# A transformer trunk on one core: layer 1's seven-product blocks put in written order, raw weights asked for earlier, and the fourth token sum moved among the first block

## The chip, the cores and the metric

The kernel runs on one core of a Trainium2 chip. The engines of the core are PE (matrix products, with its weight loads as PEld), DVE (vector), ACT (scalar and activations), POOL (a second vector engine that cannot read the product banks) and SP, which here only issues transfers. They run side by side, each through its own row of instructions, and wait for one another by semaphores. The metric is the device time of one execution in microseconds (us); lower is better. A run is stated as the median of several executions.

## The reference, cut to what matters

The model has two layers over 1024 latent tokens of width 1024. Each layer ends with a feed-forward part:

```python
def _mlp(h, w1, w2):
    return jnp.square(jax.nn.relu(h @ w1)) @ w2
...
x = x + gx2 * _mlp(_modulate(_rms(x, norm_mlp_g[i]), sx2, cx2), mlp_w1[i], mlp_w2[i])
```

`w1` is 1024 x 4096 and `w2` 4096 x 1024, all in float32. What changes lies wholly in layer 1's `_mlp`, the last part of the program.

## The kernel before

Every float32 operand of a product is held as two parts, a high part and the rest (names that end in `h` and `l`; the weights' two parts lie side by side in one tile `wsp` of 128x1024). A product of two operands is three matmuls: high by high, high by low, low by high.

Layer 1's feed-forward part has 32 feature tiles of 128. The first four go the plain way (`mlp`, whose last rows are issued by `first_done`). The other 28 go in 14 blocks, `units` 2 to 15, of two feature tiles each. A block computes its `h @ w1` as a 2x2 by 2x2 product of quarters (two feature tiles by two halves of the inner dimension, times two halves of the inner dimension by two halves of the tokens, `H0` and `H1`) with seven quarter products in place of eight. For that the tokens' quarters are combined beforehand into sums (`token_sums`: tiles t1, t2 in the buffers `oh`, `ol`, and one quarter of `mh`, `ml` overwritten; `token_sum_4`: tiles `t4`), and the weights' quarters are combined in every block (`make_s2`, four DVE operations). A quarter product (`product`) is 12 matmuls of 128x512. Below they are called P0 (`unit_head`) and P1 to P6 (`unit_tail`, in the order written); they go into three banks a, b and c. Banks are read between the products: `s1` is a copy of bank a after P0, `u2` and `u3` are bank b plus `s1`, and `added` makes the quarters c22, c21 and c12. Each of the four result quarters then goes through `squared`: a ReLU and a square on ACT (`uh`), a square on POOL, a difference on DVE (`ul`). `unit_down` multiplies the block's 256 features by `w2`: 16 banks of six matmuls, each added to the stream by one DVE operation (`residual`, L311). A block is thus 84 + 96 = 180 matmuls of 128x512.

Weights come in as raw float32 tiles of 128x1024 (`raw`, three buffers; two per block from `w1`, L1413, two from `w2`, L1435) and are cut into eleven pieces per block by `fresh`: a cast on ACT (L247), then a subtraction on POOL (L248). `makers` lists the pieces in the order of their use, `make(4)` keeps four of them made, and the tiles have four buffers: a new piece can be cast only when the piece four places before it has been used up by PE.

What sets the order: the program is written as one sequence, and a scheduler then places each engine's instructions by its own estimate of times. Only what stands in `with in_order()` keeps the written sequence, engine by engine. Before the change the blocks do not stand in it, so the scheduler interleaves products of neighbouring stages. Where a raw tile is asked for is also part of the sequence: `make_a11`, `make_s2` and `make_down` ask for it just ahead of its use. The four `token_sum_4` are written between `unit_head` of the first block and the first `unit_tail`.

## Time and profile before

| | us |
|---|---|
| median of 3 runs | 2735.89 (2733.7 to 2740.11) |
| the profiled execution: its time | 2737.96 |
| its span, by the profile | 2736.1 |
| PE busy / PEld busy | 2638.0 / 2186.3 |
| DVE / ACT / POOL busy | 1665.2 / 913.9 / 1017.1 |

Times in the rows count from the start of the span. A busy time says how long an engine had something in work, not whether it was waited for; matmuls overlap, so a single one is shown as 0.39 us long though one starts every 0.23 us. The blocks run from 2133 us to the end.

### The profile page before, as it was taken

How to read it: one execution, taken by the hardware profiler on the slowest of the kernel's cores; microseconds unless marked ns; L12 is line 12 of the kernel's file. 1: busy time of each engine (PE TensorE's matmuls, PEld its weight loads, DVE VectorE, ACT ScalarE, POOL GpSimd, SP SyncE). 2: the span in 40 equal slices, each digit the busy share in tenths (PEclk: the TensorE clock that was granted, in tenths of full speed). 3: DMA queues.
4: the chain of work that ended last, by engine and by line, in shares of the span. 5: the costliest groups of instructions: out<-in, count | busy, mean ns of one | idle time of the engine just before them, and what ended most of it. 6: DMA issues, size and time to landing. Idle time of an engine off the chain costs nothing.

```text
span 2736.1 us, 37282 instructions
## 1 busy us (share of the span) xinstructions
PE 2638.0 (96%) x13787; PEld 2186.3 (80%) x13787; DVE 1665.2 (61%) x3623; ACT 913.9 (33%) x1988; POOL 1017.1 (37%) x838
## 2 busy tenths in 40 slices
PE   7989799999999999999899999999989899999999
PEld 5878687888888888888688887788868778788787
DVE  5778779455464554624962535888877645545545
ACT  4211246121221211213532225766744232232322
POOL 3323256332332322323411002544466454454543
PEclk9999899999999999999999999999999999999999
DMA  7233420222222222311333334534221111111112
GB/s 251 72 115 124 132 82 16 63 92 81 81 96 73 85 84 78 97 43 46 97 119 116 122 118 138 166 101 136 92 66 39 39 60 48 47 55 39 62 46 85
DMA packets 148937, 239.44 MB, mean 88 GB/s; under 512 B 10460, under 2 KB 91644, under 8 KB 148756
## 3 DMA queue, kind: packets, MB, share of 16 engines
q1 hardware_dynamic: 147316, 234.45, 26.8%
q8 instruction: 108, 1.77, 0.3%
q10 hardware_dynamic: 1440, 2.62, 0.2%
q14 instruction: 73, 0.60, 0.1%
HBM read 208.71 MB, written 28.32 MB: 87 GB/s over the span
## 4 chain that ended last, share of the span: by engine, by line
PE 72%; DVE 9%; issue 3%; DMA 2%; POOL 2%; ACT 1%; DVEq 0%; POOLq 0%; SPq 0%; ACTq 0%
PE ps L295 16%; PE ps L294 16%; PE ps L296 16%; PE ps L1464 5%; PE ps L1152 3%; PE ps L1154 3%; PE ps L1153 3%; PE ps L102 3%; PE ps L1288 3%; DMA raw<-in_mlp_w_dram 2%; PE ps L1105 2%; DVE junk L218 1%; POOL wsp L248 1%; PE ps L1107 1%; DVE ny L373 1%
## 5 line engine op out<-in xcount | busy, mean ns | idle before, releaser
L248 POOL TENSOR_TENSOR wsp<-raw,wsp 128x512 fp32r<-128x512 f32 x355 | 500.0, 1413 | 938.0 <-ACT wsp L247 904.4
L311 DVE SCALAR_TENSOR_TENSOR xT<-ps,mods,xT 128x512 f32<-128x512 f32 x528 | 367.0, 711 | 308.8 <-PE ps L296 308.3
L247 ACT CAST wsp<-raw 128x512 fp32r<-128x512 f32 x368 | 224.5, 619 | 758.6 <-PE ps L296 538.7
L295 PE MATMUL ps<-ul,wsp 128*128 128x512 f32 (+1 forms) x1280 | 473.5, 370 | 1.7 <-DVE ul L1470 0.8
L218 DVE CUSTOM_DVE_ANT_0 junk<-raw,cond_b 128x256 bf16<-128x256 f32 x640 | 354.8, 554 | 192.6 <-DMA raw<-in_ada_t_dram 92.7
L296 PE MATMUL ps<-uh,wsp 128*128 128x512 f32 (+1 forms) x1280 | 468.4, 368 | 0.0
L294 PE MATMUL ps<-uh,wsp 128*128 128x512 f32 (+1 forms) x1280 | 458.9, 369 | 0.5 <-ACT wsp L247 0.5
L295 PE MATMUL ps<-ml,wsp 128*128 128x512 f32 (+1 forms) x792 | 285.5, 361 | 11.1 <-DVE ml L408 7.5
L294 PE MATMUL ps<-mh,wsp 128*128 128x512 f32 (+1 forms) x792 | 284.6, 361 | 1.2 <-ACT mh L401 1.2
L296 PE MATMUL ps<-mh,wsp 128*128 128x512 f32 (+1 forms) x792 | 283.7, 359 | 0.0
L295 PEld LDWEIGHTS ps<-ul,wsp 128*128 128x128 f32 x1280 | 241.4, 189 | 47.0 <-DVE ul L1470 7.2
L294 PEld LDWEIGHTS ps<-uh,wsp 128*128 128x128 f32 x1280 | 241.4, 189 | 41.9 <-ACT wsp L247 0.9
L296 PEld LDWEIGHTS ps<-uh,wsp 128*128 128x128 f32 x1280 | 241.2, 188 | 40.0
L966 POOL TENSOR_TENSOR tmp<-tmp 128x512 f32<-128x512 f32 (+1 forms) x104 | 103.8, 999 | 217.8 <-ACT tmp L963 189.6
L295 PEld LDWEIGHTS ps<-ml,wsp 128*128 128x128 f32 x792 | 151.1, 191 | 37.4 <-DVE ml L408 10.8
L294 PEld LDWEIGHTS ps<-mh,wsp 128*128 128x128 f32 x792 | 151.0, 191 | 24.6 <-ACT mh L401 1.4
L296 PEld LDWEIGHTS ps<-mh,wsp 128*128 128x128 f32 x792 | 151.2, 191 | 21.4
L1464 PE MATMUL ps<-mh,wsp 128*128 128x512 f32 x448 | 148.1, 397 | 14.0 <-ACT ny L1481 7.2
L963 ACT ACTIVATE tmp<-ps 128x512 f32<-128x512 f32 (+1 forms) x104 | 55.3, 532 | 257.7 <-PE ps L296 257.2
L967 DVE TENSOR_TENSOR ul<-tmp,uh 128x512 fp32r<-128x512 f32 (+1 forms) x104 | 90.5, 875 | 80.8 <-POOL tmp L966 80.8
L294 PE MATMUL ps<-hh,wsp 128*128 128x512 f32 (+1 forms) x360 | 130.0, 361 | 1.9 <-ACT wsp L247 1.6
L295 PE MATMUL ps<-hl,wsp 128*128 128x512 f32 (+1 forms) x360 | 129.5, 360 | 2.0 <-DVE hl L408 1.3
(335 smaller groups left out, 5079.0 us busy)
## 6 DMA issues: line engine op xcount, KB each, us to landing
raw<-in_mlp_w_dram SPq DMA_DIRECT2D x92, 512.0 KB, 3.5
raw<-in_ada_t_dram SPq DMA_DIRECT2D x80, 512.0 KB, 3.5
raw<-in_mlp_w_dram SPq DMA_DIRECT2D x80, 256.0 KB, 2.7
raw<-in_w_qkv_dram SPq DMA_DIRECT2D x24, 512.0 KB, 4.0
k_d<-tmp SPq DMA_DIRECT2D x40, 256.0 KB, 2.4
kh<-k_d SPq DMA_DIRECT2D x15, 640.0 KB, 5.0
kl<-k_d SPq DMA_DIRECT2D x15, 640.0 KB, 6.9
araw<-in_ada_dram SPq DMA_DIRECT2D x16, 512.0 KB, 9.6
```

Source lines behind the costliest of these rows:

```text
L102: PE.transpose(dst, src, ident[:rows, :rows])
L218: DVE.tensor_tensor_reduce(out=junk, in0=raw[:, d * 256:d * 256 + 256], in1=cond_b[:, s, :], op0=ALU.mult, op1=ALU.add, scale=1.0, scalar= ...
L247: ACT.copy(dst_hi, src)
L248: lo_eng.tensor_tensor(out=dst_lo, in0=src, in1=dst_hi.bitcast(F32), op=ALU.subtract)
L294: PE.matmul(ps, lhsT=whi, rhs=ahi, start=first, stop=False)
L295: PE.matmul(ps, lhsT=whi, rhs=alo, start=False, stop=False)
L296: PE.matmul(ps, lhsT=wlo, rhs=ahi, start=False, stop=last)
L311: DVE.scalar_tensor_tensor(out=xT[dt][ci], in0=ps, scalar=mods[l][:, 24 * k + 16 + dt, s:s + 1], in1=xT[dt][ci], op0=ALU.mult, op1=ALU.add)
L966: POOL.tensor_tensor(out=q[:, :w], in0=r[:, :w], in1=r[:, :w], op=ALU.mult)
L967: DVE.tensor_tensor(out=ul[:, off:off + w], in0=q[:, :w], in1=hs.bitcast(F32), op=ALU.subtract)
L1152: PE.matmul(ps, lhsT=ah, rhs=wh, start=(kt == 0), stop=False)
L1464: PE.matmul(ps, lhsT=a, rhs=b, start=(first and kt == 0 and n == 0), stop=(kt == 3 and n == 2), skip_group_check=True)
```

## The change

Four things are done, all in layer 1's feed-forward part.

1. All blocks stand in `with in_order()`: each engine takes their instructions as written.
2. Raw tiles are asked for earlier: `make_s1`, `make_a22`, `make_s4` and `make_down(i, 1)` issue the transfers of `up_raw(i + 1, 0)`, `down_raw(i, 0)`, `down_raw(i, 1)` and `up_raw(i + 1, 1)`; the first block's two are asked for inside `first_done`.
3. The four `token_sum_4` are written among the first `unit_tail`, one `step()` after each of u2, the first `squared`, u3 and c22.
4. One subtraction of `token_sum_4` goes from DVE to POOL, and in the first block P6 (`p3`, which needs no t4) is written ahead of P5 (`p4`), with the two weight pieces swapped to match.

```diff
@@ token_sum_4
-        DVE.tensor_tensor(out=f21, in0=f21, in1=f2, op=ALU.subtract)
+        POOL.tensor_tensor(out=f21, in0=f21, in1=f2, op=ALU.subtract)
@@ raw tiles
     def up_raw(i, j):
-        raws[i, j] = raw_w()
-        SP.dma_start(raws[i, j], mlp_w1[1][2 * i + j])
-
-    def make_a11(i):
-        up_raw(i, 0)
-        return fresh(raws[i, 0][:, H0])
+        if i in units:
+            raws[i, j] = raw_w()
+            SP.dma_start(raws[i, j], mlp_w1[1][2 * i + j])
+
+    def down_raw(i, j):
+        raws["d", i, j] = raw_w()
...
     def make_s2(i):
-        up_raw(i, 1)
...
     def make_down(i, j):
-        if j % 2 == 0:
-            raws["d", i] = raw_w()
...
+        w = fresh(raws["d", i, j // 2][:, 512 * (j % 2):512 * (j % 2) + 512])
+        if j == 1:
+            up_raw(i + 1, 1)
+        return w
+
+    def make_s1(i):
+        up_raw(i + 1, 0)
+        return fresh(sums_.pop(i))
+
+    def make_a22(i):
+        w = fresh(raws.pop((i, 1))[:, H1])
+        down_raw(i, 0)
+        return w
+
+    def make_s4(i):
+        w = fresh(raws.pop((i, 0))[:, H0])
+        down_raw(i, 1)
+        return w
@@ unit_tail
+        late = [lambda kt=kt: token_sum_4(kt) for kt in range(4)] if opens else []
+        step = lambda: late.pop(0)() if late else None
         product(b, pair_of(tsum["t2"]), True)
         DVE.tensor_tensor(out=u2, in0=b, in1=s1, op=ALU.add)
+        step()
+        us = [(big("uh"), big("ul")) for _ in range(2)]
         product(a, quarter(upper, H0), False)
         squared(tmp(), *us[0], H0, a)
+        step()
         product(b, quarter(lower, H1), False)
         DVE.tensor_tensor(out=u3, in0=b, in1=s1, op=ALU.add)
+        step()
         product(c, pair_of(tsum["t1"]), True)
         c22 = added(c, u3)
+        step()
         squared(c22, *us[1], H1, c22)
...
+        for p in (p3, p4) if opens else (p4, p3):
+            p()
@@ the end of the program
-    head = unit_head(units[0])
-    for kt in range(4):
-        token_sum_4(kt)
-    for i in units:
-        us = unit_tail(head)
-        if i + 1 in units:
-            head = unit_head(i + 1)
-        unit_down(us, store if i + 1 not in units else None)
+    with in_order():
+        head = unit_head(units[0])
+        for i in units:
+            us = unit_tail(head, i == units[0])
+            if i + 1 in units:
+                head = unit_head(i + 1)
+            unit_down(us, store if i + 1 not in units else None)
```

How this moves the instructions shows at three places. First PE inside an ordinary block, before the change. `oh` is t1 (P4), `t` is t4 (P5); the first `mh`, `ml` here are the last rows of P3, and the two after `oh` are the first rows of the next block's P0; `uh`, `ul` belong to `unit_down`.

```order
L1464 MATMUL ps<-mh_17799,wsp 128x512
L1464 MATMUL ps<-oh,wsp 128x512
L1464 MATMUL ps<-mh_17796,wsp 128x512
L1464 MATMUL ps<-ml_17804,wsp 128x512
L1464 MATMUL ps<-t_18828,wsp 128x512 x3
L1464 MATMUL ps<-t_18836,wsp 128x512 x3
L1464 MATMUL ps<-t_18844,wsp 128x512 x3
L1464 MATMUL ps<-t_18852,wsp 128x512 x3
L294 MATMUL ps<-uh,wsp 128x512
L295 MATMUL ps<-ul,wsp 128x512
```

The same place after it:

```order
L1482 MATMUL ps<-mh_17799,wsp 128x512
L1482 MATMUL ps<-oh,wsp 128x512 x12
L1482 MATMUL ps<-t_18850,wsp 128x512 x3
L1482 MATMUL ps<-t_18884,wsp 128x512 x3
L1482 MATMUL ps<-t_18910,wsp 128x512 x3
L1482 MATMUL ps<-t_18935,wsp 128x512 x3
L1482 MATMUL ps<-mh_17800,wsp 128x512
L1482 MATMUL ps<-ml_17808,wsp 128x512
```

P4 now stands in one piece, P5 follows it, and neither the next P0 nor `unit_down` reaches in between.

Second, ACT at the start of the first block, before the change (`wsp_18808` and `wsp_18811` are weight pieces of P2 and P3, `ny_18826` is s1):

```order
L247 CAST wsp_18808<-raw_18791 128x512
L247 CAST t4_18828<-tmp_18829 128x512
L247 CAST t4_18836<-tmp_18837 128x512
L247 CAST t4_18844<-tmp_18845 128x512
L247 CAST wsp_18811<-raw_18796 128x512
L247 CAST t4_18852<-tmp_18853 128x512
L1481 COPY ny_18826<-ps_18807 128x512
```

And after it (`wsp_18834`, `wsp_18862`, `wsp_18892` are the pieces s1, s4 and a22):

```order
L247 CAST wsp_18808<-raw_18721 128x512
L247 CAST wsp_18811<-raw_18723 128x512
L1499 COPY ny_18826<-ps_18807 128x512
L247 CAST wsp_18834<-tmp_18798 128x512
L247 CAST t4_18850<-tmp_18851 128x512
L247 CAST wsp_18862<-raw_18721 128x512
L1485 ACTIVATE tmp_18879<-ps_18807 128x512
L1486 ACTIVATE uh_18858<-tmp_18879 128x512
L247 CAST t4_18884<-tmp_18885 128x512
L247 CAST wsp_18892<-raw_18723 128x512
L247 CAST t4_18910<-tmp_18911 128x512
```

The copy of bank a no longer stands behind the casts of t4; those now stand between the casts of the block's own pieces.

Third, DVE in the first block. Before the change the sums of t4 stand ahead of the block, which then reads:

```order
L248 TENSOR_TENSOR t4_18852<-tmp_18853,t4_18852 128x512
L1489 TENSOR_TENSOR ny_18866<-ps_18864,ny_18826 128x512
L1470 TENSOR_TENSOR ul_18861<-tmp_18899,uh_18860 128x512
L1493 TENSOR_TENSOR ny_18867<-ps_18864,ny_18826 128x512
L1474 TENSOR_TENSOR tmp_18937<-ps_18865,ny_18867 128x512
```

After it (L1509 is u2, L1516 u3, L1492 c22; L1372 adds the two parts of a t2 tile, L248 makes the low part of a t4 tile):

```order
L1509 TENSOR_TENSOR ny_18830<-ps_18828,ny_18826 128x512
L1372 TENSOR_TENSOR tmp_18853<-ol_18494 128x512
L248 TENSOR_TENSOR t4_18850<-tmp_18851,t4_18850 128x512
L1488 TENSOR_TENSOR ul_18859<-tmp_18879,uh_18858 128x512
L1372 TENSOR_TENSOR tmp_18887<-ol_18544 128x512
L248 TENSOR_TENSOR t4_18884<-tmp_18885,t4_18884 128x512
L1516 TENSOR_TENSOR ny_18831<-ps_18828,ny_18826 128x512
L1372 TENSOR_TENSOR tmp_18913<-ol_18594 128x512
L248 TENSOR_TENSOR t4_18910<-tmp_18911,t4_18910 128x512
L1492 TENSOR_TENSOR tmp_18933<-ps_18829,ny_18831 128x512
```

Three of the four token sums now stand on DVE between u2 and c22.

## Rows read from the trace of the kernel before

**Rows 1.** PE in time: start, length, line, operation, count; rows around P0 and P1.

```profile
2119.72 0.39 PE L294 MATMUL ps<-uh,wsp 128*128 128x512 f32 x1
...
2133.09 0.39 PE L296 MATMUL ps<-uh,wsp 128*128 128x512 f32 x1
2133.32 0.39 PE L1464 MATMUL ps<-mh,wsp 128*128 128x512 f32 x1
...
2136.04 0.61 PE L1464 MATMUL ps<-ol,wsp 128*128 128x512 f32 x2
2137.02 2.58 PE L1464 MATMUL ps<-ol,wsp 128*128 128x512 f32 x10 [0.36 <-POOL wsp L248]
2146.79 0.79 PE L1464 MATMUL ps<-mh,wsp 128*128 128x512 f32 x1 [7.19 <-ACT ny L1481]
...
2151.64 0.40 PE L1464 MATMUL ps<-mh,wsp 128*128 128x512 f32 x1
...
2731.95 0.39 PE L296 MATMUL ps<-uh,wsp 128*128 128x512 f32 x1
```

**Rows 2.** Busy time by stretch: PE, PEld, DVE, ACT, POOL; granted clock, DMA, GB/s.

```profile
2147.00:2149.00 2.00, 2.00 (x5) 1.61 (x6) 0.57 (x1) 0.77 (x2) 1.67 (x2) 0.50 0.00 0
2153.00:2155.00 2.00, 2.00 (x10) 1.64 (x10) 0.00 (x0) 0.78 (x2) 1.67 (x2) 1.00 0.00 1
```

**Rows 3.** The chain of waits: start, length, what; the same cast in the first and the last block.

```profile
2157.37 0.63 ACT wsp L247
...
2704.17 0.63 ACT wsp L247
```

**Rows 4.** PE in time, in the second of the 14 blocks.

```profile
2199.29 0.39 PE L1464 MATMUL ps<-oh,wsp 128*128 128x512 f32 x1
2200.21 0.50 PE L1464 MATMUL ps<-mh,wsp 128*128 128x512 f32 x1 [0.53 <-ACT wsp L247]
...
2214.87 0.50 PE L295 MATMUL ps<-ul,wsp 128*128 128x512 f32 x1
```

**Rows 5.** DVE in time, the same block.

```profile
2209.59 0.75 DVE L1423 TENSOR_TENSOR tmp<-raw 128x512 f32<-128x512 f32 x1 [0.95 <-DMA raw<-in_mlp_w_dram]
...
2214.13 0.69 DVE L1470 TENSOR_TENSOR ul<-tmp,uh 128x512 fp32r<-128x512 f32 x1
2214.73 4.70 DVE L311 SCALAR_TENSOR_TENSOR xT<-ps,mods,xT 128x512 f32<-128x512 f32 x7
```

**Rows 6.** ACT in time: first block's start, then the second block's casts and activations.

```profile
2145.63 0.62 ACT L247 CAST t<-tmp 128x512 fp32r<-128x512 f32 x1 [5.99 <-DVE tmp L1396]
2146.16 0.58 ACT L1481 COPY ny<-ps 128x512 f32<-128x512 f32 x1
...
2204.44 0.63 ACT L1467 ACTIVATE tmp<-tmp 128x512 f32<-128x512 f32 x1
```

**Rows 7.** DVE in time while the token sums run.

```profile
2132.88 0.68 DVE L1372 TENSOR_TENSOR tmp<-ol 128x512 f32<-128x512 f32 x1
...
2141.99 1.75 DVE L1372 TENSOR_TENSOR tmp<-ol 128x512 f32<-128x512 f32 x1
```

**Rows 8.** POOL in time, the same stretch and on.

```profile
2134.43 1.30 POOL L1372 TENSOR_TENSOR tmp<-mh,ml 128x512 f32<-128x512 f32 x1 [3.29 <-DVE tmp L1396]
...
2139.80 3.38 POOL L248 TENSOR_TENSOR wsp<-raw,wsp 128x512 fp32r<-128x512 f32 x2
...
2154.58 1.04 POOL L1469 TENSOR_TENSOR tmp<-tmp 128x512 f32<-128x512 f32 x1
```

**Rows 9.** PE in time after another long idle stretch, in layer 0.

```profile
185.86 0.79 PE L294 MATMUL ps<-yh,wsp 128*128 128x512 f32 x1 [7.85 <-ACT wsp L247]
...
188.58 0.59 PE L295 MATMUL ps<-yl,wsp 128*128 128x512 f32 x1
189.01 0.40 PE L294 MATMUL ps<-yh,wsp 128*128 128x512 f32 x1
```

**Rows 10.** Line L1413, the 28 raw tiles of w1: us from issue to landing.

```profile
DMA to landing us min/median/max: 3.3/3.5/4.2
```

More of the change, by code (lines that the diff above doesn't have):

```diff
@@ L1411, in up_raw @@
     def up_raw(i, j):
-        raws[i, j] = raw_w()
-        SP.dma_start(raws[i, j], mlp_w1[1][2 * i + j])
-    def make_a11(i):
-        up_raw(i, 0)
-        return fresh(raws[i, 0][:, H0])
+        if i in units:
[3 more added lines that the diff above has]
+        raws["d", i, j] = raw_w()
+        src = mlp_w2[1, i // 2, 4 * j:4 * j + 4, :, 256 * (i % 2):256 * (i % 2) + 256]
+        SP.dma_start(raws["d", i, j].rearrange("p (m c) -> p m c", m=4), src.rearrange("m p c -> p m c"))
     def make_s2(i):
-        up_raw(i, 1)
         r1, r2 = raws[i, 0], raws[i, 1]
@@ L1431, in make_down @@
     def make_down(i, j):
-        if j % 2 == 0:
-            raws["d", i] = raw_w()
-            src = mlp_w2[1, i // 2, 2 * j:2 * j + 4, :, 256 * (i % 2):256 * (i % 2) + 256]
-            SP.dma_start(raws["d", i].rearrange("p (m c) -> p m c", m=4), src.rearrange("m p c -> p m c"))
-        return fresh(raws["d", i][:, 512 * (j % 2):512 * (j % 2) + 512])
+        w = fresh(raws["d", i, j // 2][:, 512 * (j % 2):512 * (j % 2) + 512])
[13 more added lines that the diff above has]
+        return w
     units = range(2, 16)
     for i in units:
-        makers.append(lambda i=i: make_a11(i))
+        makers.append(lambda i=i: fresh(raws[i, 0][:, H0]))
         if i > units[0]:
@@ L1445, in trunk @@
         makers.append(lambda i=i: fresh(raws[i, 1][:, H0]))
-        makers.append(lambda i=i: fresh(sums_.pop(i)))
-        makers.append(lambda i=i: fresh(raws.pop((i, 1))[:, H1]))
-        makers.append(lambda i=i: fresh(raws.pop((i, 0))[:, H0]))
+        makers.append(lambda i=i: make_s1(i))
+        if i == units[0]:
+            makers.append(lambda i=i: make_s4(i))
+            makers.append(lambda i=i: make_a22(i))
+        else:
+            makers.append(lambda i=i: make_a22(i))
+            makers.append(lambda i=i: make_s4(i))
     makers.extend(lambda j=j: make_down(units[-1], j) for j in range(4))
@@ L1482, in unit_head, with unit_tail, p4, p3 @@
         return a, s1
-    def unit_tail(head):
+    def unit_tail(head, opens):
         a, s1 = head
-        us = [(big("uh"), big("ul")) for _ in range(2)]
         b, c, u2, u3 = bank(), bank(), keep(), keep()
+        late = [lambda kt=kt: token_sum_4(kt) for kt in range(4)] if opens else []
+        step = lambda: late.pop(0)() if late else None
         product(b, pair_of(tsum["t2"]), True)
         DVE.tensor_tensor(out=u2, in0=b, in1=s1, op=ALU.add)
+        step()
+        us = [(big("uh"), big("ul")) for _ in range(2)]
         product(a, quarter(upper, H0), False)
         squared(tmp(), *us[0], H0, a)
+        step()
         product(b, quarter(lower, H1), False)
         DVE.tensor_tensor(out=u3, in0=b, in1=s1, op=ALU.add)
+        step()
         product(c, pair_of(tsum["t1"]), True)
         c22 = added(c, u3)
+        step()
         squared(c22, *us[1], H1, c22)
-        product(b, pair_of(tsum["t4"]), False)
-        c21 = added(b, s1)
-        squared(c21, *us[1], H0, c21)
-        product(c, quarter(upper, H1), False)
-        c12 = added(c, u2)
-        squared(c12, *us[0], H1, c12)
+        def p4():
+            product(b, pair_of(tsum["t4"]), False)
+            c21 = added(b, s1)
+            squared(c21, *us[1], H0, c21)
+        def p3():
+            product(c, quarter(upper, H1), False)
+            c12 = added(c, u2)
+            squared(c12, *us[0], H1, c12)
+        for p in (p3, p4) if opens else (p4, p3):
+            p()
         return us
@@ L1529, in first_done @@
                 token_sums(n // 2)
+            if n == 10:
+                up_raw(2, 0)
+                up_raw(2, 1)
         make(2)
     mlp(1, norm, (0, 1), 1, 0, first_done, 1)
-    head = unit_head(units[0])
-    for kt in range(4):
-        token_sum_4(kt)
-    for i in units:
-        us = unit_tail(head)
-        if i + 1 in units:
-            head = unit_head(i + 1)
-        unit_down(us, store if i + 1 not in units else None)
+    with in_order():
[5 more added lines that the diff above has]
+            unit_down(us, store if i + 1 not in units else None)
     ctx6.close()
```

## The prediction

> **What bounds the kernel now.** I read the page first, then the waits and the chain of waits from 2133 us on, then PE in order of time, and last the engine that PE waits for at each place where its row has a hole. PE is the bound in the stretch that changes: it starts a matmul of 128x512 every (2133.09 - 2119.72) / 59 = 0.2266 us when nothing holds it [rows 1]. The blocks are 14 x 180 = 2520 matmuls, so 571.0 us at that pace. They begin at 2133.32 and the last one starts at 2731.95 [rows 1], so 598.9 us with its own slot: 27.8 us are lost, and this is all that the change can win, since it removes no matmul. I see the loss at two places.
>
> *The opening of the first block, 10.4 us.* P1 waits 0.5 us for its weights: two matmuls from 2136.04, the next at 2137.02 instead of 2136.49. Then P2 may not add into bank a before ACT has copied it; the matmul due at 2139.29 starts at 2146.79, 7.5 us late [rows 1]. The reader is to see why: the copy needs only P0, which is over at 2136.2, but it stands in ACT's row behind the casts of t4, the last of which starts at 2145.63; the copy follows at 2146.16 [rows 6]. After that hole the granted clock is 0.50, the lower of the two levels (1.2 GHz), then 1.00 again [rows 2]: eleven steps from 2146.79 to 2151.64 take 4.85 us instead of 2.49, another 2.4 us [rows 1].
>
> *The blocks, 16.5 us.* The same cast comes at 2157.37 in the first and at 2704.17 in the last block [rows 3]: 546.8 us for 13 blocks, 42.06 each, against 180 x 0.2266 = 40.79. Of the 1.27 us, 0.7 is the hole from 2199.29 to 2200.21: the scheduler put two matmuls of the next P0 right behind P3 and P4, and their weight piece could be cast only when a buffer came free there [rows 4]. The rest lies around 2214.87, where `unit_down` waits for a `ul` [rows 4]: on DVE it comes at 2214.13, behind the weight sums that began at 2209.59 when their raw tile had landed [rows 5]. About 1 us lies in the last block; I leave that as it is.
>
> **The change, part by part.**
>
> *Written order in an ordinary block: the 1.27 us go.* I set P1's start to zero and walk the written order with the durations of the rows: product 2.72 us, ending 0.16 late for readers; ACT cast, ReLU or square 0.63 [rows 6]; POOL weight subtraction 1.3 to 1.7, square 1.04 [rows 8]; DVE 0.7, and up to 1.75 beside POOL [rows 7]. Each weight piece is cast when the product four places ahead has ended and is wanted three products later, so it has 8.2 us less about 2.2 (cast and subtraction) and less what is ahead of it on ACT and POOL, at most a ReLU, a square and POOL's square: over 3 us are left everywhere. The tightest is the second w2 piece, made at 18.4 and wanted at 21.8. The `ul` of c12, written now ahead of the weight sums, is done at 20.8 and wanted at 24.5; that of c21 at 17.6, wanted at 19.8. The weight sums wait for a raw tile that is asked for when that second piece is made (18.4) and lands 3.5 later [rows 10], at 21.9; four DVE operations bring it to 25.1. Behind them in DVE's row stand the residuals. The first is done at 25.8, and PE wants its bank, the eighth after P0's, at 28.6; they catch up at 4.70 / 7 = 0.67 each [rows 5] against 1.36 of PE. So 2.8 us of cover. If a cover fails, each us beyond it costs one us per block, 13 times. Value taken: 16.5 us won; ends 12.5 (0.3 us a block stays) and 16.5.
>
> *The opening: the copy comes at once, but c22 comes late.* The copy follows P0 by 0.1 us, so P2 and, with all pieces of P1 to P3 made earlier, P3 and P4 run on: the 0.5 + 7.5 + 2.4 = 10.4 us go. But P6, now the product after P4, adds into bank c and must wait until DVE has read c22, and c22 stands in DVE's row behind three token sums, each a round over DVE, POOL, ACT and DVE. P1 to P4 end on schedule, so P6 is due at 2133.32 + 60 x 0.2266 = 2146.9. The walk, with 0.05 us at each hand-over: u2 is done at 2139.6 (P1's end 2138.9 + 0.69). Round one: t2's two parts 1.2 (between 0.68 alone and 1.75 beside POOL [rows 7], and POOL is busy for half of it), POOL's subtraction 1.3 [rows 8], cast 0.6 [rows 6]: 2142.8. The second round begins only behind the first `squared` in DVE's row: cast of the piece s4, ReLU, POOL's subtraction 1.3 and square 1.04, `ul` 0.7: 2146.5; then 1.2 + 1.3 + 0.6: 2149.7. The third needs on ACT the cast of a22, on POOL its subtraction 1.3 and the sum of mh and ml 1.3, then 1.3 and a cast: 2155.1. Low part 0.7 and c22 0.7, and P6 starts at 2156.7. That is 9.8 us late, a longer hole than the one removed. The moved subtraction lies on this path three times (0.6 us more each on POOL than DVE's 0.68). Ends: with DVE never held by POOL 2155.1; with POOL at 1.7 [rows 8] in the seven or eight operations on the path 2159.5.
>
> Rows 7 and 8 show DVE's sum of t2 taking 1.75 from 2141.99 beside a POOL run that ends at 2143.18: it ended 0.56 after POOL did, about its length alone. The Trainium skill, "SBUF — State Buffer", section "SBUF: two separate sides", says that a DVE operation with two SBUF inputs and a GpSimd operation that reads SBUF lock each other out for a whole instruction. It speaks against handing a subtraction to POOL in a stretch where DVE sums too: by it the third round's sum holds POOL up by a further 0.7 us and P6 starts at 2157.4, the sum below would be 0.7 us worse; the row agrees with it.
>
> The hole costs clock again. After 7.2 us idle 2.4 us were lost [rows 1]; after 7.85 us idle in layer 0 the steps of 0.43 instead of 0.23 last from 185.86 to 189.01 [rows 9], some 1.6 us lost (half of 3.15). I take 2.4, from the nearer place; ends 1.6 and 3.5. And P5 is now last before P0 and `unit_down`: c21 stands on DVE behind c12's `ul`, its own `ul` is done at 2169.4, and the fifth matmul of `unit_down` wants it at 2168.1: 1.3 us, ends 0 and 2.5. The opening then loses 9.8 + 2.4 + 1.3 = 13.5 us, ends 9.8 and 18.6, against 10.4 before.
>
> *At nothing:* the raw tiles of the first block asked for earlier (in the rows before the change they did not hold PE there), the order of the stores (the last still follows the last residual), and SP, whose row holds the same transfers in the same number.
>
> **The sum.** -16.5 - 10.4 + 13.5 = -13.4 us. The profiled execution, 2737.96 us, would become 2724.6; it stands 2.07 above the median, so on the median 2735.89 - 13.4 = 2722.5 us.
>
> **The rivals.**
>
> *The opening is cheaper than reckoned.* For it: the two rows on DVE's sum differ by 1.07 us, and most of POOL's work may fall beside ACT. P6 at 2155.1 (8.2 late), 1.6 of clock, no wait for c21: 9.8 us, so -16.5 - 10.4 + 9.8 = -17.1 and 2718.8. Against it: POOL has eight operations on the path.
>
> *The blocks keep half of their loss.* Written order makes every engine wait for the oldest instruction; if a `ul` or a weight piece comes 0.6 us late in each block, 13 x 0.6 = 7.8 us stay, and the time is 2730. For it: the hole is now in the scheduler's order and a fixed order cannot fill any. Against it: the covers of 2 to 4 us above.
>
> *Slower: the raw tile at the head of DVE's row.* DVE stands still until the tile has landed, with eight residuals behind it, and PE runs out of banks. The cover is 2.8 us; the time passes 2741 when each block loses (13.4 + 5.5) / 13 = 1.5 us, that is when the tile lands 4.3 us later than reckoned, 7.8 us after its issue. The longest of 28 took 4.2 [rows 10]; for it speaks only that the buffer comes free through POOL's row, which is longer in time than I know. At 2 us a block it gives 2748.
>
> *It changes nothing that counts.* Were the opening at its worst (18.6) and 0.3 us kept per block, -12.5 - 10.4 + 18.6 = -4.3, 2731.6; with a little more of either, 2734.
>
> **How the numbers follow.** Forecast as summed, 2722.5: 0.63 (2720 to 2728). Cheaper opening, 2718.8: 0.13. Half the loss kept, 2730: 0.12, of which half is faster by over 0.2%. No change, 2734: 0.05. Slower, 2748: 0.07. The range takes in the first three but their outer edges: 2717 to 2731. 0.2% is 5.5 us, about what a measurement of this kernel can tell from no change: faster (under 2730.4) 0.63 + 0.13 + 0.06 = 0.82; within 0.06 + 0.05 = 0.11; slower 0.07.
>
> **What would show it.** In the profile after, blocks of 40.8 us from one to the next and PE without holes in them; s1's copy within 0.2 us of P0; one hole of about 10 us before P6 of the first block, ended by DVE's c22, with the lower clock behind it; a wait of about 1 us for the last `ul` at the first `unit_down`. Wrong would be: holes that end on DVE L311 in every block (the slower rival), holes that end on ACT or POOL pieces (half the loss kept), or P6 held by something other than c22.

## The result, and the profile after

| | before | after |
|---|---|---|
| median, same chip, 6 runs each (us) | 2735.80 | 2756.69 |
| ratio, 95% interval | | 1.0073 [1.0063, 1.0084] |
| P0 of the first block to the last matmul (us) | 598.6 | 619.0 |
| one block to the next (us) | 42.05 | 42.54 |

The change makes the kernel 20.9 us slower; 2722.5 had been forecast, with 2717 to 2731 as the range. The third line of the table is the measure that I use below. The instructions ahead of the blocks are the same in both kernels (a few right ahead of P0 in another order), but the start of P0 moves by some us from execution to execution (2133.32 in the profile of before, 2127.83 in that of after), and counting from P0 leaves that out. By it the change costs 20.4 us. Counted from the last matmul of one `unit_down` to that of the next, the first block (from P0) is 9.95 us longer than before, the next twelve are 5.9 longer together (0.49 each), and the last is 4.55 longer. At PE's pace the 2520 matmuls of the blocks take 571.0 us, so 48.2 us are lost in the blocks after the change, against 27.8 before.

PE of the changed kernel in order of time (start, length, line, operation, count, and in brackets how long PE stood idle and what ended it). L1482 is a quarter product, L294 to L296 are `unit_down`:

```profile
2127.83 0.39 PE L1482 MATMUL ps<-mh,wsp 128*128 128x512 f32 x1
...
2138.71 2.88 PE L1482 MATMUL ps<-oh,wsp 128*128 128x512 f32 x12
2151.46 0.76 PE L1482 MATMUL ps<-mh,wsp 128*128 128x512 f32 x1 [9.87 <-DVE tmp L1492]
...
2155.88 2.89 PE L1482 MATMUL ps<-t,wsp 128*128 128x512 f32 x12
...
2161.77 0.39 PE L296 MATMUL ps<-uh,wsp 128*128 128x512 f32 x1
2166.45 0.80 PE L294 MATMUL ps<-uh,wsp 128*128 128x512 f32 x1 [4.29 <-ACT uh L1486]
2169.33 0.79 PE L295 MATMUL ps<-ul,wsp 128*128 128x512 f32 x1 [2.09 <-DVE ul L1488]
...
2175.42 0.39 PE L294 MATMUL ps<-uh,wsp 128*128 128x512 f32 x1
...
2214.00 0.50 PE L295 MATMUL ps<-ul,wsp 128*128 128x512 f32 x1 [0.79 <-DVE ul L1488]
...
2265.81 0.50 PE L294 MATMUL ps<-uh,wsp 128*128 128x512 f32 x1 [0.27 <-DVE xT L311]
...
2681.99 0.50 PE L295 MATMUL ps<-ul,wsp 128*128 128x512 f32 x1 [0.79 <-DVE ul L1488]
...
2721.61 0.49 PE L294 MATMUL ps<-uh,wsp 128*128 128x512 f32 x1 [0.82 <-ACT uh L1486]
2724.49 0.51 PE L295 MATMUL ps<-ul,wsp 128*128 128x512 f32 x1 [2.39 <-DVE ul L1488]
...
2728.48 0.39 PE L296 MATMUL ps<-uh,wsp 128*128 128x512 f32 x1
...
2746.86 0.39 PE L296 MATMUL ps<-uh,wsp 128*128 128x512 f32 x1
```

Read against [rows 1, 4], there are three places of loss.

- **First block, 21.7 us (11.8 before: the opening's 10.4 and what an ordinary block lost).** P1 to P4 run without a hole, so P6 is due at 2138.71 + 12 x 0.2267 = 2141.43 and starts at 2151.46: 10.0 us, ended by DVE's c22. Its 12 matmuls then take 4.42 us instead of 2.72: 1.7 us. At the first `unit_down` PE waits for c21, first for `uh` (due 2162.00, 4.45 us late), then for `ul` (due 2166.68, 2.65 us), and from 2169.33 to 2175.42 makes 14 steps in 6.09 us instead of 3.17: 2.9 us.
- **Ordinary blocks.** The same wait for `ul` comes at 2214.00 and at 2681.99, 11 blocks later: 467.99 / 11 = 42.54. In each block PE loses 0.95 us for c21's `ul` and 0.43 us (0.27 of it idle, at 2265.81) for a bank that the residual (L311) has not read yet, and the rest of the 1.75 us above 40.79 in steps a little longer than 0.2267.
- **Last block, 5.3 us (about 1 before).** 0.98 for `uh`, 2.65 for `ul`, and ten steps from 2724.49 to 2728.48 in 3.99 us instead of 2.27, 1.7 us.

21.7 + 12 x 1.75 + 5.3 = 48.0, the 48.2 that are lost. Behind the two holes of the first block the granted clock is at its lower level. The table of stretches gives stretch, busy time of PE, PEld, DVE, ACT and POOL, granted clock (1.00 is 2.4 GHz, 0.50 is 1.2 GHz), DMA share and GB/s, as in [rows 2]:

```profile
2152.00:2154.00 2.00, 2.00 (x6) 1.59 (x5) 0.41 (x1) 0.00 (x0) 1.92 (x2) 0.50 0.00 0
2155.00:2158.00 3.00, 3.00 (x15) 2.47 (x14) 0.80 (x2) 2.22 (x4) 1.18 (x2) 1.00 0.00 0
2170.00:2172.00 2.00, 2.00 (x6) 1.57 (x5) 1.97 (x3) 0.00 (x0) 0.41 (x1) 0.50 0.28 70
```

Why is c21 late in every block? DVE in one of them (L1492 is the add that reads a quarter out of its bank, L1488 the `ul`, L1424 and L1425 begin the weight sums):

```profile
2246.72 0.69 DVE L1492 TENSOR_TENSOR tmp<-ps,ny 128x512 f32<-128x512 f32 x1 [0.66 <-PE ps L1482]
2249.89 1.75 DVE L1488 TENSOR_TENSOR ul<-tmp,uh 128x512 fp32r<-128x512 f32 x1 [2.48 <-POOL tmp L1487]
2251.57 0.68 DVE L1492 TENSOR_TENSOR tmp<-ps,ny 128x512 f32<-128x512 f32 x1
2254.72 1.76 DVE L1488 TENSOR_TENSOR ul<-tmp,uh 128x512 fp32r<-128x512 f32 x1 [2.48 <-POOL tmp L1487]
2256.41 0.68 DVE L1492 TENSOR_TENSOR tmp<-ps,ny 128x512 f32<-128x512 f32 x1
...
2261.26 1.78 DVE L1424 TENSOR_TENSOR tmp<-raw 128x512 f32<-128x512 f32 x1
```

ACT (L1485 ReLU, L1486 square into `uh`) and POOL (L1487 its own square, L248 a weight subtraction) in the same stretch:

```profile
2247.45 0.63 ACT L1485 ACTIVATE tmp<-tmp 128x512 f32<-128x512 f32 x1 [2.78 <-DVE tmp L1492]
2248.11 0.63 ACT L1486 ACTIVATE uh<-tmp 128x512 fp32r<-128x512 f32 x1
```

```profile
2248.82 1.04 POOL L1487 TENSOR_TENSOR tmp<-tmp 128x512 f32<-128x512 f32 x1 [2.20 <-ACT uh L1486]
2249.82 1.28 POOL L248 TENSOR_TENSOR wsp<-raw,wsp 128x512 fp32r<-128x512 f32 x1
```

The three views together are one chain: add 0.69 (2246.72), ReLU 0.63, ACT's square 0.63, POOL's square 1.04, `ul` 1.75, and only then the next quarter's add (2251.57). That is 4.85 us from add to add, while PE delivers a quarter every 2.72. DVE idles 2.48 us in each round of the chain; in the second of them the next add (due at 2252.16, as reckoned below) stands ready behind the `ul` all the while. P4 ended at 2246.72, so P5 had ended 2.72 later, at 2249.44, and P6 at 2252.16: c21's add is 2.1 us late, c12's add 4.3. In the kernel before, DVE's row has the next quarter's add ahead of the `ul`, and the add waits for PE alone (the second block; DVE, then POOL):

```profile
2203.72 0.69 DVE L1474 TENSOR_TENSOR tmp<-ps,ny 128x512 f32<-128x512 f32 x1 [2.74 <-PE ps L1464]
2204.33 0.68 DVE L1470 TENSOR_TENSOR ul<-tmp,uh 128x512 fp32r<-128x512 f32 x1
```

```profile
2204.47 1.69 POOL L248 TENSOR_TENSOR wsp<-raw,wsp 128x512 fp32r<-128x512 f32 x1 [0.69 <-DVE tmp L1474]
```

The `ul` has a second trouble: it starts 0.07 us after POOL's subtraction and takes 1.75 instead of 0.69. In the rows just shown it starts 0.14 us ahead, and it is POOL that takes long. After the change all 56 `ul` are long (one of them beside a token sum of POOL); the view of one line gives shortest, middle and longest duration in ns, here of L1488 after, then of its twin L1470 before:

```profile
L1488 DVE TENSOR_TENSOR ul<-tmp,uh x56: 1732/1760/1767, 2140.1 to 2727.5; 128x512 fp32r<-128x512 f32 x56
```

```profile
L1470 DVE TENSOR_TENSOR ul<-tmp,uh x56: 681/684/694, 2155.7 to 2717.3; 128x512 fp32r<-128x512 f32 x56
```

### The profile page after: what moved, and what is told of

Its sections match the earlier page's. It is cut to its first block, busy times and chain, and to the rows that moved or that the text cites. A ratio compares the mean times of both kernels' runs of the same rounds, so it can differ in the third digit from the quotient of the medians.

```text
span 2751.0 us, 37292 instructions
## 1 busy us (share of the span) xinstructions
PE 2639.5 (96%) x13787; PEld 2186.2 (79%) x13787; DVE 1703.1 (62%) x3619; ACT 911.0 (33%) x1988; POOL 1011.6 (37%) x842
## 4 chain that ended last, share of the span: by engine, by line
PE 68%; DVE 9%; issue 6%; POOL 5%; ACT 2%; DMA 1%; POOLq 0%; SPq 0%; DVEq 0%; ACTq 0%
PE ps L294 16%; PE ps L295 15%; PE ps L296 15%; PE ps L1152 3%; PE ps L1154 3%; PE ps L1153 3%; PE ps L102 3%; PE ps L1288 3%; POOL wsp L248 3%; POOL tmp L1487 2%; PE ps L1482 2%; PE ps L1105 2%; DVE junk L218 1%; PE ps L1107 1%; DVE ul L1488 1%
## 5 line engine op out<-in xcount | busy, mean ns | idle before, releaser
L248 POOL TENSOR_TENSOR wsp<-raw,wsp 128x512 fp32r<-128x512 f32 x355 | 495.0, 1401 | 873.9 <-ACT wsp L247 844.5
L311 DVE SCALAR_TENSOR_TENSOR xT<-ps,mods,xT 128x512 f32<-128x512 f32 x528 | 362.8, 710 | 286.1 <-PE ps L296 285.6
L294 PE MATMUL ps<-uh,wsp 128*128 128x512 f32 (+1 forms) x1280 | 474.3, 372 | 8.3 <-ACT uh L1486 5.1
L296 PE MATMUL ps<-uh,wsp 128*128 128x512 f32 (+1 forms) x1280 | 473.0, 370 | 0.0
L295 PE MATMUL ps<-ml,wsp 128*128 128x512 f32 (+1 forms) x792 | 285.4, 361 | 10.4 <-DVE ml L408 7.5
L294 PEld LDWEIGHTS ps<-uh,wsp 128*128 128x128 f32 x1280 | 242.6, 190 | 55.4 <-DVE xT L311 8.3
L294 PE MATMUL ps<-mh,wsp 128*128 128x512 f32 (+1 forms) x792 | 283.8, 360 | 1.2 <-ACT mh L401 1.2
L296 PE MATMUL ps<-mh,wsp 128*128 128x512 f32 (+1 forms) x792 | 283.6, 359 | 0.0
L296 PEld LDWEIGHTS ps<-uh,wsp 128*128 128x128 f32 x1280 | 242.3, 189 | 40.1
L1488 DVE TENSOR_TENSOR ul<-tmp,uh 128x512 fp32r<-128x512 f32 x56 | 98.4, 1758 | 162.4 <-POOL tmp L1487 162.4
L294 PEld LDWEIGHTS ps<-mh,wsp 128*128 128x128 f32 x792 | 150.9, 191 | 24.6 <-ACT mh L401 1.4
L296 PEld LDWEIGHTS ps<-mh,wsp 128*128 128x128 f32 x792 | 151.0, 191 | 21.1
L1482 PE MATMUL ps<-mh,wsp 128*128 128x512 f32 x448 | 144.2, 392 | 9.9 <-DVE tmp L1492 9.9
L294 PE MATMUL ps<-hh,wsp 128*128 128x512 f32 (+1 forms) x360 | 128.8, 358 | 2.5 <-ACT wsp L247 2.2
```

The source lines that it names most:

```text
L248: lo_eng.tensor_tensor(out=dst_lo, in0=src, in1=dst_hi.bitcast(F32), op=ALU.subtract)
L294: PE.matmul(ps, lhsT=whi, rhs=ahi, start=first, stop=False)
L295: PE.matmul(ps, lhsT=whi, rhs=alo, start=False, stop=False)
L296: PE.matmul(ps, lhsT=wlo, rhs=ahi, start=False, stop=last)
L311: DVE.scalar_tensor_tensor(out=xT[dt][ci], in0=ps, scalar=mods[l][:, 24 * k + 16 + dt, s:s + 1], in1=xT[dt][ci], op0=ALU.mult, op1=ALU.add)
L1482: PE.matmul(ps, lhsT=a, rhs=b, start=(first and kt == 0 and n == 0), stop=(kt == 3 and n == 2), skip_group_check=True)
```

## The experiments

Three explanations stood against each other. **A**: written order puts the next quarter's add on DVE behind the `ul` of the quarter before, and the quarters become one chain. **B**: the token sums among the first block cost the time. **C**: the raw tiles or the subtraction given to POOL do. All ratios below are to the kernel before on the same chip, with 95% intervals; the last two columns are from the one profiled execution of each.

| run | median us | ratio | P0 to last matmul | block to block |
|---|---|---|---|---|
| before | 2735.36 to 2737.32, by chip | 1 | 598.6 | 42.05 |
| after | 2756.69 | 1.0073 [1.0063, 1.0084] | 619.0 | 42.54 |
| no_order | 2729.21 | 0.9968 [0.9956, 0.9980] | 591.4 | 42.04 |
| order_only | 2745.61 | 1.0033 [1.0021, 1.0046] | 611.1 | 42.55 |
| sums_ahead | 2755.04 | 1.0066 [1.0053, 1.0078] | 619.0 | 42.55 |
| lag | 2725.29 | 0.9955 [0.9941, 0.9969] | 588.8 | 40.80 |
| own_tile | 2723.39 | 0.9953 [0.9940, 0.9965] | 585.3 | 40.80 |
| piece_first | 2736.87 | 1.0002 [0.9993, 1.0011] | 600.4 | 40.92 |
| staged | 2721.54 | 0.9941 [0.9929, 0.9954] | 582.5 | 40.80 |
| mixed | 2714.28 | 0.9915 [0.9902, 0.9929] | 576.6 | 40.80 |
| raw_late | 2722.84 | 0.9954 [0.9939, 0.9969] | 586.9 | 40.80 |
| own_mixed | 2718.82 | 0.9936 [0.9921, 0.9951] | 580.2 | 40.80 |
| no_swap | 2716.70 | 0.9936 [0.9919, 0.9952] | 579.1 | 40.80 |
| dve_sub | 2753.80 | 1.0064 [1.0049, 1.0079] | 616.2 | 42.55 |

### no_order: the change without the written order

```diff
-    with in_order():
+    with nullcontext():
```

> The changed kernel with one thing undone: the scheduler orders the blocks again; raw tiles asked for early, token sums written among the first block, POOL's subtraction and the exchange of P5 and P6 in the first block all stay. Theory A (the written order puts the next quarter's add on DVE behind the ul of the quarter before, so the quarters form one chain of 4.8 us each): from the third block on DVE's row has the adds of c22 and c21 next to each other again, blocks fall from 42.54 to 42.1 or less, the two holes of 0.95 and 0.43 us in each block go, the last block loses about 1 us instead of 5; total 2736 to 2744, some 10 us of the 20.9 gone. Rival B (the token sums among the first block cost nearly all of it, blocks included, because they shift everything behind them): blocks stay at 42.5, 2750 to 2757. Rival C (raw tiles or POOL's subtraction): as B, no change.

It measured 2729.2, below the range for A: all of the 20.9 us go, and some 7 more. Blocks are back at 42.04 from the third on, with the kernel before's hole for a weight piece in them, as in [rows 4]. PE in one of them:

```profile
2319.19 0.50 PE L1482 MATMUL ps<-mh,wsp 128*128 128x512 f32 x1 [0.53 <-ACT wsp L247]
```

B and C fall as causes by themselves: all their parts are in this kernel, though the scheduler places them. The 7 us under the kernel before lie in the opening, where the 7.5 us hole behind the casts of t4 is gone. So the rest of the change is a gain, as long as the scheduler sets the order.

### order_only: the written order without the rest

```diff
+    with in_order():
         head = unit_head(units[0])
         for kt in range(4):
             token_sum_4(kt)
```

> The kernel before with one part alone: the blocks in written order, with the four token sums ahead of the first block's tail; raw tiles asked for late, DVE's subtraction in the token sums, P5 ahead of P6. On DVE the only difference in a steady block is that the ul of c22 stands ahead of the add of c21, and the ul of c12 ahead of the weight sums. Theory A: blocks at 42.5 with the holes of the changed kernel (0.95 for c21's ul, 0.4 for the residual), 5 us in the last block; in the first block u2 stands behind four token sums, so P3 waits about 6 us with some 2 us of low clock, in place of the 7.5 + 2.4 of before: total 2744 to 2750. Rival B: blocks as before or better, total 2724 to 2736. Rival C (the raw tile is what counts): blocks above 43, since DVE's residuals stand behind the wait for the tile, 2755 and more.

2745.6, within A's range; blocks 42.55, and PE in a middle block has the two holes of the changed kernel to the hundredth:

```profile
2294.76 0.50 PE L295 MATMUL ps<-ul,wsp 128*128 128x512 f32 x1 [0.79 <-DVE ul L1470]
...
2304.03 0.50 PE L294 MATMUL ps<-uh,wsp 128*128 128x512 f32 x1 [0.27 <-DVE xT L311]
```

A alone makes the loss of the repeated blocks (5.95 us over twelve, against 5.9) and of the last one (4.5). The raw tiles are asked for late here and the blocks take as long as in the changed kernel, so the early request is not their cause. The first block is only 1.9 us longer than in the kernel before, although the hole before P3 is 9.0 us where I had put about 6.

### sums_ahead: the token sums in front again

```diff
-        late = [lambda kt=kt: token_sum_4(kt) for kt in range(4)] if opens else []
+        if opens:
+            for kt in range(4):
+                token_sum_4(kt)
+        late = []
```

> The changed kernel with one thing undone: the four token sums stand in front of the first block's tail again instead of among its products; written order, early raw tiles, POOL's subtraction and P6 ahead of P5 in the first block stay. Theory A: the hole of 10 us before P6 goes, but u2 now stands behind four sums and P3 waits 6 to 9 us, with 2 us of low clock; the waits for c21 at the first unit_down (4.5 for uh, 2.7 for ul) stay or shrink a little since the written order makes them; blocks stay at 42.5; total 2748 to 2757. Rival B (the sums among the first block cause the loss): 2736 to 2746.

2755.0, in A's range. PE in the first block:

```profile
2147.50 0.80 PE L1482 MATMUL ps<-mh,wsp 128*128 128x512 f32 x1 [10.40 <-DVE ny L1512]
...
2170.15 0.80 PE L295 MATMUL ps<-ul,wsp 128*128 128x512 f32 x1 [2.38 <-DVE ul L1488]
```

The hole only moves, from c22 (10.0 us) to u2 (10.6 us, a little more than I had put). The waits for c21 at the first `unit_down` stay: 2.0 us for `uh` (4.45 in the changed kernel) and the same 2.65 for `ul`. The kernel of written order alone, which keeps P5 ahead of P6, has one wait of 0.95 us for c21 there. By these rows it is P5 in the last place, right ahead of P0 and `unit_down`, that leaves c21's chain without cover. That is argued, not shown: the two kernels differ by 9.4 us (8.0 from P0 on), but also by POOL's subtraction, which dve_sub below puts at 2.9, and by the early requests; the exchange alone in written order was not run.

### lag: each `ul` one place later on DVE

```diff
-        DVE.tensor_tensor(out=ul[:, cs], in0=r, in1=uh[:, cs].bitcast(F32), op=ALU.subtract)
+        rest.append(lambda: DVE.tensor_tensor(out=ul[:, cs], in0=r, in1=uh[:, cs].bitcast(F32), op=ALU.subtract))
...
+    def low():
+        rest.pop(0)()
```

`low()` is called behind u3, behind the adds of c21 and c12, and behind the next block's P0.

> The changed kernel with each quarter's ul written one place later on DVE, behind the next quarter's add (c11's behind u3, c22's behind the add of c21, c21's behind the add of c12, the last one behind the next block's P0); everything else stays, the token sums among the first block too. Theory A: each quarter's add comes as soon as its product ends, the holes in the blocks go, the period falls from 42.54 to 40.8 to 41.2 (13 blocks: 17 to 22 us), the last block loses about 1 us instead of 5, the first unit_down waits 1 to 3 us instead of 7.1; the hole of about 10 us before P6 stays, with its 2 us of clock; total 2722 to 2732. Rival B: blocks stay at 42.5 and the total at 2750 or more. Rival C (DVE and POOL share time, not order): blocks improve by under 0.5, 2745 to 2755.

2725.3, 31.4 us less than the changed kernel, by the place of four instructions in one engine's row. DVE of a block:

```profile
2241.37 0.69 DVE L1497 TENSOR_TENSOR tmp<-ps,ny 128x512 f32<-128x512 f32 x1 [2.03 <-PE ps L1482]
2241.98 1.60 DVE L1488 TENSOR_TENSOR ul<-tmp,uh 128x512 fp32r<-128x512 f32 x1
2244.09 0.69 DVE L1497 TENSOR_TENSOR tmp<-ps,ny 128x512 f32<-128x512 f32 x1 [0.51 <-PE ps L1482]
...
2247.26 1.76 DVE L1488 TENSOR_TENSOR ul<-tmp,uh 128x512 fp32r<-128x512 f32 x1 [0.96 <-POOL tmp L1487]
```

Now the adds wait for PE and come every 2.72 us; three of a block's four `ul` still take 1.6 to 1.76 (the fourth 0.86), and the blocks have no hole. So changing the place in the row is enough; the long `ul` by itself makes PE wait for nothing in these blocks once no add stands behind it. What is left is the first block (a hole of 9.9 us before P6, 2.8 us for c21's `ul`) and 1.55 us in the last.

### own_tile: POOL's square not in place

```diff
-        POOL.tensor_tensor(out=r, in0=r, in1=r, op=ALU.mult)
-        DVE.tensor_tensor(out=ul[:, cs], in0=r, in1=uh[:, cs].bitcast(F32), op=ALU.subtract)
+        sq = tmp()
+        POOL.tensor_tensor(out=sq, in0=r, in1=r, op=ALU.mult)
+        DVE.tensor_tensor(out=ul[:, cs], in0=sq, in1=uh[:, cs].bitcast(F32), op=ALU.subtract)
```

> The changed kernel with POOL's square written to a tile of its own, so that it need not wait until ACT's square has read the tile that it overwrites; written order and everything else stay. Theory A, that a quarter is a chain (add 0.69, ReLU 0.63, ACT's square 0.63, POOL's square 1.04, ul 1.76, with hand-overs 4.83) that the next quarter's add waits for: each quarter gets about 0.6 us shorter, 4.2. c21's ul stands behind two such quarters and comes 1.2 us earlier, which is more than its hole of 0.95, so blocks fall from 42.54 to about 40.9; in the last block and at the first unit_down 1 to 2 us remain to be waited for. Total 2728 to 2740. If the order on DVE costs nothing by itself (rival B or C): within 3 us of the changed kernel.

2723.4, better than my range, because two links of the chain got shorter, not one. DVE, then POOL, of a block:

```profile
2244.45 0.68 DVE L1493 TENSOR_TENSOR tmp<-ps,ny 128x512 f32<-128x512 f32 x1
2247.02 0.69 DVE L1489 TENSOR_TENSOR ul<-tmp,uh 128x512 fp32r<-128x512 f32 x1 [1.88 <-POOL tmp L1488]
2247.63 0.68 DVE L1493 TENSOR_TENSOR tmp<-ps,ny 128x512 f32<-128x512 f32 x1
```

```profile
2245.94 1.04 POOL L1488 TENSOR_TENSOR tmp<-tmp 128x512 f32<-128x512 f32 x1 [0.26 <-ACT tmp L1485]
2247.05 1.81 POOL L248 TENSOR_TENSOR wsp<-raw,wsp 128x512 fp32r<-128x512 f32 x1
```

POOL's square now follows the ReLU instead of ACT's square, as meant. But POOL's subtraction now starts 0.03 us after the `ul` instead of 0.07 before it, and it is POOL that takes long (1.81), the `ul` 0.69. A quarter is 3.18 us (2244.45 to 2247.63) instead of 4.85. That is still a chain, and still slower than PE's 2.72, but short enough to stay under the cover of P0 and the first matmuls of `unit_down`.

### piece_first: the weight subtraction ahead of the square on POOL

```diff
         for kt, (bh, bl) in enumerate(bs):
...
+        make(4)
```

The line stands in `product`, behind its 12 matmuls.

> The changed kernel with the next weight piece made right behind a product's matmuls, that is ahead of the quarter's ReLU on ACT and ahead of its square on POOL; DVE's order does not change. In the changed kernel POOL starts a weight subtraction of 1.28 us at the same moment as DVE the ul, and the ul takes 1.76. If the two hold each other up (theory A's fifth link), the ul falls to about 0.7, the ReLU comes 0.6 later, a quarter takes about 3.9 instead of 4.83, c21's ul comes about 2 us earlier and the blocks fall to about 40.9: total 2728 to 2740. The Trainium skill, SBUF - State Buffer, section SBUF: two separate sides, has a DVE operation with two SBUF inputs and a GpSimd operation lock each other out for a whole instruction; by it the ul falls to its length alone. If the ul is long for another reason, it stays at 1.76, the chain gets 0.6 longer, and the total is 2760 or more.

The total (2736.9) and the blocks (40.92) are as expected of the chain with a shorter `ul`, but the reason is only half shown: the `ul` fell to 0.69 where a quarter is in time, and stayed at 1.76 where the chain is still late. DVE:

```profile
2256.02 0.69 DVE L1489 TENSOR_TENSOR ul<-tmp,uh 128x512 fp32r<-128x512 f32 x1 [2.48 <-POOL tmp L1488]
...
2259.79 1.76 DVE L1489 TENSOR_TENSOR ul<-tmp,uh 128x512 fp32r<-128x512 f32 x1 [2.48 <-POOL tmp L1488]
```

POOL:

```profile
2256.32 1.55 POOL L248 TENSOR_TENSOR wsp<-raw,wsp 128x512 fp32r<-128x512 f32 x1 [0.33 <-ACT wsp L247]
...
2259.72 1.29 POOL L248 TENSOR_TENSOR wsp<-raw,wsp 128x512 fp32r<-128x512 f32 x1
```

Each time the operation that started first kept its length or nearly so and the other one waited. In a steady block c22's `ul` is one that is short: with it the quarter takes 3.78 us from add to add instead of 4.85, and the block's hole for c21's `ul` is gone, though DVE's order is that of the changed kernel. Together with lag this says that in these blocks it takes both, the order and the long `ul`, to make PE wait. In the first block the edit made the hole before P6 longer, 12.1 us instead of 10.0; I did not follow that up.

### staged: the lagged kernel with its token sums in stages

```diff
-        step()
+        if opens:
+            rest.append(t4_high(1, f))
...
+            squared(c22, *us[1], H1, c22)
+            f = t4_open(3)
+            low()
```

`t4_open` is POOL's sum, `t4_high` DVE's two steps and the cast, and the low part of t4 goes through `low()` one place later.

> The lagged kernel (2725.3) with the token sums of the first block written in stages as well: POOL's sum of a token tile ahead of a product, DVE's two steps and ACT's cast one place later, the low part one place later again, c22's add ahead of the third and fourth sum, the subtraction on DVE. Theory A with its second part (in the first block the hole of 10 us before P6 is c22 standing on DVE behind three whole token sums): the hole falls to 0 to 4 us, most of the low clock behind it goes too, the rest as lagged: 2713 to 2722. If the hole comes from POOL's or DVE's load and not from the place in the row, it stays above 6 us: 2722 to 2727.

2721.5, at the upper end of what I expected. The hole of 9.9 us before P6 fell to 2.1, but a new one of 3.3 stands inside P5, before its last three matmuls, for the fourth t4 (PE):

```profile
2149.68 0.47 PE L1496 MATMUL ps<-mh,wsp 128*128 128x512 f32 x1 [1.95 <-DVE tmp L1511]
...
2159.49 0.51 PE L1496 MATMUL ps<-t,wsp 128*128 128x512 f32 x1 [3.15 <-ACT t L1402]
```

c22 behind three sums was the cause of most of that hole (1.9 us of it can be the subtraction, which is back on DVE here; see dve_sub); with it gone, the fourth sum is late next.

### mixed: first block to the scheduler, the others lagged and in written order

```diff
-    with in_order():
-        head = unit_head(units[0])
-        for i in units:
-            us = unit_tail(head, i == units[0])
+    head = unit_head(units[0])
+    us = unit_tail(head, True)
+    head = unit_head(units[1])
+    low()
+    unit_down(us)
+    with in_order():
+        for i in units[1:]:
+            us = unit_tail(head, False)
```

> The lagged kernel (2725.3) with its first block left to the scheduler, as in the run without written order, and the other 13 blocks lagged and in written order. The two parts should add: the first block loses about 5 us (run without written order) instead of 16.5 (lagged), the blocks run at 40.9 as lagged: 2711 to 2718. If the scheduler's first block leaves the second one late in its ul or weights, some of it stays: 2718 to 2725.

2714.3, 0.85% below the kernel before and the fastest of all; 576.6 us from P0 to the last matmul, 5.8 lost against PE's pace. ACT's copy of s1 marks the blocks; from the third block to the last it is 448.79 / 11 = 40.80:

```profile
2199.57 0.59 ACT L1504 COPY ny<-ps 128x512 f32<-128x512 f32 x1 [0.19 <-PE ps L1482]
...
2648.36 0.59 ACT L1504 COPY ny<-ps 128x512 f32<-128x512 f32 x1 [0.19 <-PE ps L1482]
```

The two parts add as A has it.

### raw_late, own_mixed, no_swap, dve_sub: the other parts of the change

raw_late takes the early requests out of own_tile (`up_raw` and `down_raw` are called where the first piece is made, as before the change).

> The own-tile kernel (2723.4, blocks without holes) with the raw weights asked for where they were before the change, each when its first piece is made. In the blocks of the run with written order alone, the transfers of the raw tiles stand at the same distance from DVE's adds as in the changed kernel (4.32 us before them at both places looked at), so the early request only waits for its buffer: the time stays at 2721 to 2727. If a tile's landing does hold ACT's cast or DVE's weight sums once the quarters no longer hide it, each block loses 0.5 us or more: 2730 and up.

2722.8 against 2723.4, blocks 40.80: the early request is worth nothing in the repeated blocks, also where the chain does not hide it. In the two profiled executions the first block is 1.6 us longer without it (58.8 against 57.2); the medians do not show this.

own_mixed is own_tile with its first block left to the scheduler, as in mixed, without the lag.

> The own-tile kernel with the first block left to the scheduler and the other 13 in written order, without the lag. The first block should lose about 5 us (run without written order) instead of the 14 of the own-tile kernel, the last one almost nothing (0.3 there against 1.5 in the lagged and mixed kernels): 2711 to 2715, at or a little under the mixed kernel (2714.3). If the scheduler's first block comes out worse with the further tile: 2715 to 2722.

2718.8, outside the first range: the further tile changes the scheduler's first block for the worse (PE is late by 1.3, 0.9, 1.5 and 1.1 us for t twice, for an add and for `ul`), and mixed stays ahead. Why the scheduler chose so I did not look into.

no_swap is own_mixed with P5 ahead of P6 in the first block, the two weight pieces with it.

> The kernel of the run beside it (own tile, first block left to the scheduler) with P5 ahead of P6 in the first block's text as before the change, to see what the exchange alone is worth. PE's order within a priority is then c21 first, and its product needs all four token sums: if the sums are done late, PE waits 2 to 6 us for them in the first block, since the scheduler has only c12's product and the next block's P0 to put there: 2713 to 2720. If the scheduler fills the gap: within 2 us of the run beside it.

2716.7 against 2718.8, 579.1 against 580.2 us from P0: no difference that I would read anything into. Under the scheduler the exchange is worth nothing.

dve_sub is the changed kernel with one line undone:

```diff
-        POOL.tensor_tensor(out=f21, in0=f21, in1=f2, op=ALU.subtract)
+        DVE.tensor_tensor(out=f21, in0=f21, in1=f2, op=ALU.subtract)
```

> The changed kernel with the subtraction in the token sums back on DVE. By the prediction's walk POOL's subtraction lies three times on the path to c22, 0.6 us longer each than DVE's: the hole before P6 falls from 10.0 to about 8.2 us, the blocks do not change: 2753 to 2756. If POOL's part runs beside other work there, the hole stays at 10; if DVE is the fuller of the two in this stretch, it grows to 11 or 12: 2757 to 2760.

2753.8, and PE starts P6 8.15 us late instead of 10.0, as reckoned:

```profile
2155.38 0.76 PE L1482 MATMUL ps<-mh,wsp 128*128 128x512 f32 x1 [7.99 <-DVE tmp L1492]
```

The subtraction on POOL costs what its rows say, and this part of C is in the loss: the first block is 2.9 us shorter, the others are as in the changed kernel.

## Why the prediction was wrong, point by point

- **The bound, and what could be won: right.** PE's pace and 27.8 us of loss; mixed loses 5.8 us, at the same pace.
- **s1's copy and P1 to P4: right.** They run on without a hole, so the 7.5 + 0.5 + 2.4 us go.
- **P6 behind c22: right, place, cause and size.** 9.8 us reckoned, 10.0 measured; the share of POOL's subtraction (0.6 x 3) is the 1.85 us that dve_sub gives back. The clock behind it was put at 2.4 and took 1.7. DVE of the changed kernel shows c22 (2150.63) behind the low part of the third sum:

```profile
2150.02 0.69 DVE L248 TENSOR_TENSOR t<-tmp,t 128x512 fp32r<-128x512 f32 x1 [3.14 <-ACT t L247]
2150.63 0.68 DVE L1492 TENSOR_TENSOR tmp<-ps,ny 128x512 f32<-128x512 f32 x1
...
2157.90 1.76 DVE L1488 TENSOR_TENSOR ul<-tmp,uh 128x512 fp32r<-128x512 f32 x1 [1.62 <-POOL tmp L1487]
2159.58 0.68 DVE L1492 TENSOR_TENSOR tmp<-ps,ny 128x512 f32<-128x512 f32 x1
```

- **"The 1.27 us go": wrong, and it is the step that failed.** The walk put c21's add at P5's end and its `ul` at 17.6, wanted at 19.8. In the written order c22's `ul` stands in DVE's row between the two, so the add came 2.1 us later and the `ul`, beside POOL, took 1.07 us longer: 17.6 + 3.2 = 20.8, which is what the rows show (2256.48 counted from P4's end at 2246.72, that is 11.04 on the walk's scale). The cover of 2.2 us was thus gone, and a hole of 0.95 us came in its place, in every block. Two things were left out, and either alone would have fitted under the cover: as an estimate from the rows, the order with a `ul` of 0.69 makes the add 1.1 us late (a quarter of 3.78 against 2.72), and the longer `ul` alone is 1.07. piece_first and lag, which take away one of the two each, have no such hole. The residuals, behind c12's late `ul` and the weight sums, lost their cover too (0.43). Ordinary blocks: 12 x (42.54 - 40.79) = 21.0 us of the miss.
- **"1.3 us at the first `unit_down`": too small.** I had seen that c21 stands behind c12's `ul`, but not that c12's add stands behind c22's `ul`, itself behind the fourth token sum: P6 ends at about 2156, its add comes at 2159.58 (rows above). 7.1 us, and the clock falls once more for 2.9. The clock behind P6 gave 0.7 back. In all the opening lost 21.7 us, not 13.5: 8.2 us of the miss.
- **The last block "as it is": wrong by 4.3 us.** No next P0 stands between c12 and `unit_down` there, so c21's chain has less cover than in any other block.
- **Together** 21.0 + 8.2 + 4.3 = 33.5 of the 34.2 us between forecast and result.
- **The rivals.** "Half the loss kept" had the right general reason (written order waits for the oldest instruction) and even named a late `ul`, but set its price at 0.6 us a block from covers that were not there. The slower rival had the right sign for a wrong cause: its sign, a hole that ends on L311 in every block, is there (2265.81), but L1424 starts the weight sums behind a `ul` without waiting for a transfer in the changed kernel, and raw_late shows no cost in the blocks. The exchange brings nothing under the scheduler, and in written order it leaves c21 last.
- **The rule of the skill.** The Trainium skill, "SBUF — State Buffer", section "SBUF: two separate sides", says that the operation that starts first gets the shared ports for the whole instruction. I weighed it for the token sums alone, where it would have added 0.7 us. The rows of after and of own_tile agree with it at a place where I had not looked, the `ul` beside the weight subtraction: 1.75 us when DVE starts 0.07 later, 0.69 when it starts 0.03 earlier.

What is not settled: why piece_first lengthens the hole before P6; how much of the first block's loss is the exchange of P5 and P6, which was not undone alone in written order; and how the order and the long `ul` share the losses of the first and the last block.

## What to carry to other kernels

When a row is to be fixed in written order, walk it by the engine, not by the product: an instruction that waits for a round over other engines (here `ul`, four hand-overs after its add) must not stand ahead of one that only waits for PE and frees a bank. Written one place later, the same order gains 1.25 us in each block here instead of costing 0.5. And check each fixed place apart: the scheduler was worse by 1.25 us in each repeated block, yet better by more than 10 us in the first, so the best kernel fixes the one and leaves the other.
